# HGRN scores within a chunk: six levels computed in blocks of 32 tokens with 32-column weights, kept in a compact matrix and put in place by ScalarE

## The chip, the cores and the metric

The kernel runs on one core of one Trainium2 chip. Its time is the time of one execution on the device in microseconds (us). The engines are TensorE (PE, whose weight loads are shown apart as PEld), VectorE (DVE), ScalarE (ACT), GpSimd (POOL) and SyncE (SP, which issues most DMAs).

## The reference, cut to what the change touches

The program is a decoder trunk of two layers over 1024 tokens of width 1024. Layer 0 mixes tokens by HGRN2, layer 1 by a gated linear recurrence, and each is followed by a SwiGLU feed-forward block. The change touches the score part of HGRN2 alone, which is, for each of 8 heads with 128 keys:

```python
rel = bb[:, :, :, None, :] - bb[:, :, None, :, :]          # bb: running sum of log f over the tokens
decay = jnp.exp(jnp.where(causal, rel, -jnp.inf))
scores = jnp.einsum('bhtk,bhtsk,bhsk->bhts', qb, decay, kb)
o = jnp.einsum('bhts,bhsv->bhtv', scores, vb) + jnp.einsum('bhtk,bhkv->bhtv', qb * jnp.exp(bb), state)
```

The score of a query at token t and a key at token s carries the product of the forget factors f between them, for each key dimension apart, so it isn't one matrix product.

## The kernel before

**Tiling.** Activations stand transposed, 128 features on the partitions and 512 tokens (a half of the sequence) along the row. A head and a half make one unit: there are 8 x 2 = 16 of them. `unit` makes the projections f, q and g of a head by `gemm` (L275 to L282): three products of fp32r halves for each of 8 row blocks, 128x512 each, so that fp32 accuracy comes out of them. Then it starts a `core` (the function that the change edits).

**The levels.** A core handles 4 chunks of 128 tokens (CPH = 4) by eight levels. Level 0 is a product of keys and queries for the diagonal alone (L485). Levels m = 1, 2, 4, ..., 64 join neighbouring blocks of m tokens: queries in the second half of each pair of blocks against keys in its first half. Up to m = 32 a level is, for each chunk, one full fp32 product: all 128 keys of the chunk are the weights, the 64 queries in second halves are what moves through (L501). Of the 128x64 result only the blocks of that level are wanted, and VectorE copies them under a mask into the score matrix `at` (128 keys x 4 chunks x 128 queries) by COPY_PREDICATED (L532; L486 for level 0). At m = 64 the weights are the 64 keys of the first half alone, the result stands on partitions 0 to 63 (L514), and ScalarE puts it in place (L536). After each level's product VectorE multiplies the keys `kt` and queries `qp` by the running decay products, so it waits for the product, and the next level's product waits for it. A product of fp32 shows in the trace as two pairs of weight load (LDWEIGHTS) and MATMUL, so a level of 4 products is 8 pairs.

**Order.** A core is a generator. Each `gemm` step advances a count of nanoseconds (`tick`), and a core's next level is written out once its count has come up (G_LV = 1300 per level). The instructions of TensorE keep the order in which they are written, so a level of small products stands between 128x512 products of the projections of another head or half. Masks are made once by GpSimd (`make_mask`) behind the first unit's values. After the last level the keys are transposed (L543), the state is updated (L552 and the lines behind it), and the output is the product of `at` with the values (L566).

Of the kernel before, what the change touches and what calls it, by code (L numbers as in the profile page):

```python
# [9 lines left out]
F32 = mybir.dt.float32  # L10
F32R = mybir.dt.float32r
I32 = mybir.dt.int32
U8 = mybir.dt.uint8
AF = mybir.ActivationFunctionType
ALU = mybir.AluOpType
P = 128
H = 512
EPS = 1e-6
GELU_C = 0.7978845608028654
N_ST, N_OUT = 7000.0, 1500.0  # L20
N_T = 1000.0
# [26 lines left out]
def tile_trunk(  # L48
# [23 lines left out]
    nc = tc.nc  # L72
# [3 lines left out]
    CPH = H // P  # L76
# [39 lines left out]
    def pe(ins):  # L116
        return keep(ins)
# [3 lines left out]
    make_identity(nc, ident[:])  # L121
    ones = cp.tile([P, P], F32, name="ones")
    nc.vector.memset(ones[:], 1.0)
    identi = cp.tile([P, P], U8, name="identi")
    nc.vector.tensor_copy(identi[:], ident[:])
    masks = {}

    def make_mask(m):
        mf = t2k("D", f"mf{m}")[:, :P]
        keep(nc.gpsimd.memset(mf, 0.0))  # L130
        v = mf.rearrange("p (b h m) -> p b h m", h=2, m=m)[:, :, 1, :]
        keep(nc.gpsimd.memset(v, 1.0))
        nb = P // (2 * m)
        keep(
            nc.gpsimd.affine_select(
                out=v, in_=v, pattern=[[-2 * m, nb], [0, m]], compare_op=ALU.is_ge, fill=0.0, base=0, channel_multiplier=1
            )
        )
        keep(
            nc.gpsimd.affine_select(  # L140
                out=v, in_=v, pattern=[[2 * m, nb], [0, m]], compare_op=ALU.is_ge, fill=0.0, base=m - 1, channel_multiplier=-1
            )
        )
        mi = cp.tile([P, P], U8, name=f"mask{m}")
        keep(nc.gpsimd.tensor_copy(mi[:], mf))
        masks[m] = mi

# [317 lines left out]
    def hgrn(norms, after):  # L467
# [2 lines left out]
        operand, side, second, factors, raws, first_cols, loads = norms  # L470
        ws0, omlb = [], []
        ats = [sp.tile([P, CPH, P], F32, tag="slab", name=f"at{i}", bufs=BUFS["slab"]) for i in range(2)]
        n_at = [0]
        state = {}

        def core(h, half, hd, qt, ft, kt, vt, sink, flags):


            nm = f"{h}_{half}"
            ct = lambda a, c: a[:, c * P : (c + 1) * P]  # L480
            at = ats[n_at[0] % 2]
            n_at[0] += 1
            lv = psb(f"lv0_{nm}")
            for c in range(CPH):
                pe(mm(ct(lv, c), ct(kt, c), ct(qt, c), start=True, stop=True))  # L485
            nc.vector.copy_predicated(  # L486
                at[:], identi[:].unsqueeze(1).to_broadcast([P, CPH, P]), lv[:].rearrange("p (c t) -> p c t", t=P)
            )
            qp = t2k("D", f"qp_{nm}")
            tt(qp[:], qt[:], ft[:], ALU.mult)  # L490
            yield G_LV
            Tt = slab(f"T_{nm}")
            T, off, m = ft[:], 0, 1
            while m < P:
                lv = psb(f"lv{m}_{nm}")
                if m < 64:
                    second = lambda a: a.rearrange("p (b h m) -> p b h m", h=2, m=m)[:, :, 1, :]
                    lvc = lambda c: lv[:, c * 64 : (c + 1) * 64]
                    for c in range(CPH):
                        pe(  # L500
                            mm(  # L501
                                lvc(c).rearrange("p (b m) -> p b m", m=m),
                                ct(kt, c),
                                second(ct(qp, c)),
                                start=True,
                                stop=True,
                            )
                        )
                    sel = at[:].rearrange("p c (b h m) -> p c b h m", h=2, m=m)[:, :, :, 1, :]
                    msk = second(masks[m][:]).unsqueeze(1).to_broadcast([P, CPH, P // (2 * m), m])  # L510
                else:
                    for c in range(CPH):
                        pe(
                            mm(  # L514
                                lv[0:64, c * 64 : (c + 1) * 64],
                                kt[:, c * P : c * P + 64],
                                qp[:, c * P + 64 : (c + 1) * P],
                                start=True,
                                stop=True,
                            )  # L520
                        )
                n2 = H // (2 * m)
                Tv = T.rearrange("p (n h) -> p n h", h=2)
                qv = qp[:].rearrange("p (n h m) -> p n h m", h=2, m=m)[:, :, 1, :]
                kv = kt[:].rearrange("p (n h m) -> p n h m", h=2, m=m)[:, :, 0, :]
                tt(kv, kv, Tv[:, :, 1:2].to_broadcast([P, n2, m]), ALU.mult)
                tt(qv, qv, Tv[:, :, 0:1].to_broadcast([P, n2, m]), ALU.mult)
                Tn = Tt[:, off : off + n2]
                off += n2
                tt(Tn, Tv[:, :, 0], Tv[:, :, 1], ALU.mult)  # L530
                if m < 64:
                    nc.vector.copy_predicated(  # L532
                        sel, msk, lv[:, : CPH * 64].rearrange("p (c b m) -> p c b m", c=CPH, m=m)
                    )
                else:
                    nc.scalar.copy(at[0:64, :, 64:P], lv[0:64, : CPH * 64].rearrange("p (c t) -> p c t", t=64))  # L536
                T, m = Tn, 2 * m
                yield G_LV


            pk = psb(f"pk_{nm}")
            for c in range(CPH):
                pe(nc.tensor.transpose(ct(pk, c), ct(kt, c), ident[:]))  # L543
            kT = slab(f"kT_{nm}")
            act(kT[:], pk[:], AF.Copy)
            yield G_PK
            pu = psb(f"pu_{nm}")
            vs = lambda c: vt[c // 2][:, (c % 2) * 2 * P + hd * P : (c % 2) * 2 * P + (hd + 1) * P]
            Ss = [state.get(h)]
            St = slab(f"S_{nm}")  # L550
            for c in range(CPH):
                pe(mm(ct(pu, c), ct(kT, c), vs(c), start=True, stop=True))  # L552
            for c in range(CPH):
                if half == NHALF - 1 and c == CPH - 1:
                    continue
                S1 = ct(St, c)
                if Ss[-1] is None:
                    nc.vector.tensor_copy(S1, ct(pu, c))
                else:
                    stt(S1, Ss[-1], T[:, c : c + 1], ct(pu, c), ALU.mult, ALU.add)  # L560
                Ss.append(S1)
            state[h] = Ss[-1]
            yield G_PU
            po = psb(f"po_{nm}")
            for c in range(CPH):
                pe(mm(ct(po, c), at[:, c, :], vs(c), start=True, stop=Ss[c] is None))  # L566
                if Ss[c] is not None:
                    pe(mm(ct(po, c), ct(qp, c), Ss[c], start=False, stop=True))

            sq = t2k("A", f"osq_{nm}")  # L570
            act(sq[:], po[:], AF.Square)
            ss = sp.tile([P, CPH], F32, tag="ss", name=f"ss_{nm}")
            nc.vector.tensor_reduce(
                ss[:], sq[:].rearrange("p (c v) -> p c v", v=P), mybir.AxisListType.X, ALU.add
            )
            rs = rsqrt(f"o{nm}", ss[:], 1.0 / P, CPH)
            on = slab(f"on_{nm}")
            tt(
                on[:].rearrange("p (c v) -> p c v", v=P),
                po[:].rearrange("p (c v) -> p c v", v=P),  # L580
                rs.unsqueeze(2).to_broadcast([P, CPH, P]),
                ALU.mult,
            )
            flags["tail"] = True
            yield G_PL if h == NH - 1 and half else G_PO
            while "g" not in flags:
                yield 600.0
            pt = psb(f"pt_{nm}")
            for c in range(CPH):
                pe(nc.tensor.transpose(ct(pt, c), ct(on, c), ident[:]))  # L590
            og = t2k("B", f"og_{nm}")
            stt(og[:], pt[:], pc("hn", 0), flags["g"][:], ALU.mult, ALU.mult)
            sink[half] = split(f"o{nm}", og[:])
# [145 lines left out]
        for h in range(NH):  # L739
# [5 lines left out]
            if hd == 0:  # L745
                wv = value_weights(hp) if h else []
                if h == 0:
                    vts = [values_start(wv)]
                    for m in (1, 2, 4, 8, 16, 32):
                        make_mask(m)  # L750
                    for a in ats:
                        keep(nc.gpsimd.memset(a[:], 0.0))
                    factors.job = start(second())
                else:
                    vts = [values(hp, half, wv) for half in range(NHALF)]
# [851 lines left out]
```

## Time and profile before

| what | us |
|---|---|
| median of 3 runs (lowest, highest) | 2274.61 (2270.29, 2275.03) |
| profiled execution: its own time | 2269.08 |
| profiled execution: span of the core | 2267.4 |
| TensorE busy | 2224.9 |
| TensorE weight loads busy | 1868.1 |
| VectorE busy | 1628.9 |
| ScalarE busy | 936.1 |
| GpSimd busy | 840.5 |

Busy time of TensorE is the union of its matmuls, whose ends are modelled, so it is not a share of its peak. The HGRN units run from about 50 us to 606 us of the span; the rest is the feed-forward blocks and the second layer, which the change leaves alone. Columns of the views are named where the rows stand.

### The profile page before, as it was taken

How to read it: one execution, taken by the hardware profiler on the slowest of the kernel's cores; microseconds unless marked ns; L12 is line 12 of the kernel's file. 1: busy time of each engine (PE TensorE's matmuls, PEld its weight loads, DVE VectorE, ACT ScalarE, POOL GpSimd, SP SyncE). 2: the span in 40 equal slices, each digit the busy share in tenths (PEclk: the TensorE clock that was granted, in tenths of full speed). 3: DMA queues.
4: the chain of work that ended last, by engine and by line, in shares of the span. 5: the costliest groups of instructions: out<-in, count | busy, mean ns of one | idle time of the engine just before them, and what ended most of it. 6: DMA issues, size and time to landing. Idle time of an engine off the chain costs nothing.

```text
span 2267.4 us, 31380 instructions
## 1 busy us (share of the span) xinstructions
PE 2224.9 (98%) x11022; PEld 1868.1 (82%) x11022; DVE 1628.9 (72%) x2667; ACT 936.1 (41%) x1559; POOL 840.5 (37%) x603
## 2 busy tenths in 40 slices
PE   8999999999999999999999999998999999999998
PEld 8898898898887888888888887877887888888887
DVE  7676758758888776766666767767987777675666
ACT  6223122222353333333544365567733333345444
POOL 4102011012206775654324333234056766543240
PEclk9999999999999999999999999999999999999999
DMA  5013123212444555444776111111645645447762
GB/s 150 28 48 112 56 66 103 80 61 75 154 167 158 188 188 161 156 156 154 279 258 221 43 38 47 47 56 56 209 135 191 198 155 172 141 156 283 260 203 76
DMA packets 279072, 310.94 MB, mean 137 GB/s; under 512 B 18953, under 2 KB 166530, under 8 KB 278914
## 3 DMA queue, kind: packets, MB, share of 16 engines
q1 hardware_dynamic: 278914, 308.94, 41.7%
q8 instruction: 86, 1.41, 0.3%
q14 instruction: 72, 0.59, 0.1%
HBM read 216.07 MB, written 92.80 MB: 136 GB/s over the span
## 4 chain that ended last, share of the span: by engine, by line
PE 86%; DVE 8%; ACT 3%; issue 1%; DMA 1%; SPq 0%; POOL 0%; DVEq 0%; ACTq 0%; POOLq 0%
PE pa L279 8%; PE pa L280 8%; PE pa L281 8%; PE pb L279 4%; PE pb L280 4%; PE pb L281 4%; PE lv L501 3%; PE pc L279 3%; PE pc L281 3%; PE pc L280 3%; PE pg L279 2%; PE pg L280 2%; PE pg L281 2%; PE pd L281 1%; PE pd L280 1%; PE pd L279 1%
## 5 line engine op out<-in xcount | busy, mean ns | idle before, releaser
L1119 POOL TENSOR_TENSOR s<-raw_fi,raw_fi 128x512 f32<-128x512 f32 x40 | 57.9, 1448 | 283.4 <-DMA raw_fi<-in_ffn_w_in_dram 274.2
L93 DVE TENSOR_TENSOR lo_a<-raw_fi,hi_a 128x512 fp32r<-128x512 f32 x116 | 117.7, 1016 | 43.9 <-ACT hi_a L93 43.9
L93 DVE TENSOR_TENSOR lo_s<-s,hi_s 128x512 fp32r<-128x512 f32 x80 | 93.4, 1168 | 75.4 <-ACT hi_s L93 75.1
L279 PE MATMUL pa<-hi_x,hi_w 128*128 128x512 f32 (+1 forms) x364 | 139.7, 384 | 0.0
L281 PE MATMUL pa<-hi_x,lo_w 128*128 128x512 f32 (+1 forms) x364 | 139.1, 382 | 0.0
L280 PE MATMUL pa<-lo_x,hi_w 128*128 128x512 f32 (+1 forms) x364 | 139.1, 382 | 0.0
L93 DVE TENSOR_TENSOR lo_x<-ld_t,hi_x 128x512 fp32r<-128x512 f32 x88 | 87.0, 997 | 56.0 <-ACT hi_x L93 37.1
L204 POOL TENSOR_TENSOR lo_w<-ld_s,hi_w 128x512 fp32r<-128x512 f32 x44 | 69.0, 1569 | 150.6 <-ACT hi_w L93 103.2
L93 ACT ACTIVATE hi_a<-raw_fi 128x512 fp32r<-128x512 f32 x116 | 72.8, 627 | 123.5 <-PE pc L280 76.7
L279 PE MATMUL pa<-hi_t_n,hi_s 128*128 128x512 f32 x304 | 119.6, 394 | 3.1 <-ACT u L93 1.5
L280 PE MATMUL pa<-lo_t_n,hi_s 128*128 128x512 f32 x304 | 118.4, 389 | 0.0
L281 PE MATMUL pa<-hi_t_n,lo_s 128*128 128x512 f32 x304 | 118.4, 389 | 0.0
L501 PEld LDWEIGHTS lv<-qp,k 128*128 128x128 f32 x768 | 98.6, 191 | 8.8 <-issue 1.5
L279 PE MATMUL pb<-hi_x,hi_w 128*128 128x512 f32 x264 | 102.7, 389 | 0.0
L280 PE MATMUL pb<-lo_x,hi_w 128*128 128x512 f32 x264 | 102.7, 389 | 0.0
L281 PE MATMUL pb<-hi_x,lo_w 128*128 128x512 f32 x264 | 102.7, 389 | 0.0
L501 PE MATMUL lv<-qp,k 128*128 128x64 f32 x768 | 96.5, 268 | 1.3 <-DVE qp L93 1.2
L204 POOL TENSOR_TENSOR lo_f<-raw_f,hi_f 128x512 fp32r<-128x512 f32 x14 | 18.3, 1311 | 211.6 <-DMA wls<-lo_was 88.8
L93 ACT ACTIVATE hi_s<-s 128x512 fp32r<-128x512 f32 x80 | 50.6, 632 | 108.1 <-PE pa L280 76.3
L93 DVE TENSOR_TENSOR lo_s<-raw_fi,hi_s 128x512 fp32r<-128x512 f32 x80 | 94.9, 1186 | 0.1
L93 ACT ACTIVATE hi_w<-ld_s 128x512 fp32r<-128x512 f32 x88 | 55.3, 628 | 78.7 <-PE pb L280 24.5
L93 ACT ACTIVATE hi_s<-raw_fi 128x512 fp32r<-128x512 f32 x80 | 50.2, 628 | 79.5 <-PE pd L280 57.0
(398 smaller groups left out, 7289.4 us busy)
## 6 DMA issues: line engine op xcount, KB each, us to landing
raw_fi<-in_ffn_w_in_dram SPq DMA_DIRECT2D x160, 256.0 KB, 3.2
da<-in_ffn_w_out_dram SPq DMA_DIRECT2D x88, 256.0 KB, 3.9
ld_a<-in_ffn_w_out_dram SPq DMA_DIRECT2D x66, 256.0 KB, 4.8
xd<-xT SPq DMA_DIRECT2D x32, 256.0 KB, 2.5
xT<-xd SPq DMA_DIRECT2D x32, 256.0 KB, 4.8
hb22d<-c SPq DMA_DIRECT2D x22, 256.0 KB, 3.3
ht3d<-c SPq DMA_DIRECT2D x22, 256.0 KB, 2.7
ht2d<-c SPq DMA_DIRECT2D x22, 256.0 KB, 2.0
```

What stands on the lines that cost most here:

```text
L93: ins = f(*args, **kwargs)
L204: ins = (lo_engine.tensor_tensor if lo_engine else tt)(lo[:], src, hi[:], ALU.subtract)
L279: pe(mm(pt, wh, xh, start=st[0], stop=False, skip_group_check=skip))
L280: pe(mm(pt, wh, xl, start=False, stop=False, skip_group_check=skip))
L281: pe(mm(pt, wl, xh, start=False, stop=st[1], skip_group_check=skip))
L501: mm(lvc(c).rearrange("p (b m) -> p b m", m=m), ct(kt, c), second(ct(qp, c)), start=True, stop=True,)
L1119: add(s1, a21, a22, ALU.add)
```

## The change

A block length BL = 32 is introduced. For level 0 and the levels m = 1 to 16 the new helper `within` takes each chunk in four blocks of 32 tokens: 32 keys are the weights, the 32 queries of the same block (level 0) or the 16 of them in second halves (m = 1 to 16) move through, and the result goes to the 32 partitions of those keys. A level is then 16 products where it was 4. Level m = 32 becomes, for each chunk, two products of 32 keys by 32 queries (8 products where there were 4). Level m = 64 stays as it was: 4 products of 64 keys by 64 queries.

The results of levels 0 to 16 go by COPY_PREDICATED into a new compact matrix `ad` (128 x 4 x 32), a quarter of `at`; the masks and the identity shrink to 32 columns. After level 16 ScalarE copies `ad` in four pieces of 32 partitions onto the diagonal of `at`, and level 32 goes into `at` by two ScalarE copies, without VectorE and without a mask. GpSimd makes five masks, each cut out by four copies, and the identity by four, and clears `ad` too.

```diff
+    identi = cp.tile([P, BL], U8, name="identi")
     masks = {}
+
+    def own_columns(o, src):
+        for b in range(0, P, BL):
+            keep(nc.gpsimd.tensor_copy(o[b : b + BL, :], src[b : b + BL, b : b + BL]))
...
+        ads = [cp.tile([P, CPH, BL], F32, name=f"ad{i}") for i in range(2)]
...
             lv = psb(f"lv0_{nm}")
-            for c in range(CPH):
-                pe(mm(ct(lv, c), ct(kt, c), ct(qt, c), start=True, stop=True))
+
+            def within(q, n):
+
+                for c in range(CPH):
+                    for b in range(0, P, BL):
+                        t = slice(c * P + b, c * P + b + BL)
+                        o, qs = lv[b : b + BL, c * n : (c + 1) * n], q(t)
+                        if len(qs.shape) == 3:
+                            o = o.rearrange("p (b m) -> p b m", m=qs.shape[2])
+                        pe(mm(o, kt[:, t], qs, start=True, stop=True))
+
+            within(lambda t: qt[:, t], BL)
             nc.vector.copy_predicated(
-                at[:], identi[:].unsqueeze(1).to_broadcast([P, CPH, P]), lv[:].rearrange("p (c t) -> p c t", t=P)
+                ad[:],
+                identi[:].unsqueeze(1).to_broadcast([P, CPH, BL]),
+                lv[:, : CPH * BL].rearrange("p (c t) -> p c t", t=BL),
             )
...
-                if m < 64:
+                if m < BL:
                     second = lambda a: a.rearrange("p (b h m) -> p b h m", h=2, m=m)[:, :, 1, :]
-                    lvc = lambda c: lv[:, c * 64 : (c + 1) * 64]
+                    within(lambda t: second(qp[:, t]), BL // 2)
+                    sel = ad[:].rearrange("p c (b h m) -> p c b h m", h=2, m=m)[:, :, :, 1, :]
+                    msk = second(masks[m][:]).unsqueeze(1).to_broadcast([P, CPH, BL // (2 * m), m])
+                else:
+
                     for c in range(CPH):
...
+                        for b in range(0, P, 2 * m):
+                            k0, q0 = c * P + b, c * P + b + m
+                            o = lv[b : b + m, c * m : (c + 1) * m]
+                            pe(mm(o, kt[:, k0 : k0 + m], qp[:, q0 : q0 + m], start=True, stop=True))
...
-                if m < 64:
+                if m < BL:
                     nc.vector.copy_predicated(
-                        sel, msk, lv[:, : CPH * 64].rearrange("p (c b m) -> p c b m", c=CPH, m=m)
+                        sel, msk, lv[:, : CPH * BL // 2].rearrange("p (c b m) -> p c b m", c=CPH, m=m)
                     )
+                    if 2 * m == BL:
+                        for b in range(0, P, BL):
+                            nc.scalar.copy(at[b : b + BL, :, b : b + BL], ad[b : b + BL, :, :])
                 else:
-                    nc.scalar.copy(at[0:64, :, 64:P], lv[0:64, : CPH * 64].rearrange("p (c t) -> p c t", t=64))
+                    for b in range(0, P, 2 * m):
+                        src = lv[b : b + m, : CPH * m].rearrange("p (c t) -> p c t", t=m)
+                        nc.scalar.copy(at[b : b + m, :, b + m : b + 2 * m], src)
```

On TensorE, where head 0's second half (names `_0_1`) runs its level m = 16 between two steps of a 128x512 projection (`pg`), there stands before:

```order
L280 MATMUL pg_0_1213<-lo_x_0_149,hi_g_0_1098 128x512
L281 MATMUL pg_0_1213<-hi_x_0_148,lo_g_0_1099 128x512
L501 MATMUL lv_0_1_1217<-qp_1_1120,k_1_891 128x64 x4
L279 MATMUL pg_0_1213<-hi_x_1_159,hi_g_0_1098 128x512
L280 MATMUL pg_0_1213<-lo_x_1_160,hi_g_0_1098 128x512
```

and in the changed kernel:

```order
L284 MATMUL pg_0_1369<-lo_x_0_150,hi_g_0_1194 128x512
L285 MATMUL pg_0_1369<-hi_x_0_149,lo_g_0_1195 128x512
L499 MATMUL lv_0_1_1373<-qp_1_1228,k_1_966 32x16 x16
L283 MATMUL pg_0_1369<-hi_x_1_160,hi_g_0_1194 128x512
L284 MATMUL pg_0_1369<-lo_x_1_161,hi_g_0_1194 128x512
```

The level stands at the same place; 4 products of 64 moving columns have become 16 of 16 columns, each with its own weights.

On ScalarE, around the end of the same core (the copies into `at_`), there stands before:

```order
L93 ACTIVATE k_0_1106<-k_0_1106 128x512
L93 ACTIVATE sg_q_0_1209<-q_0_1164 128x512
L536 COPY at_136<-lv_0_1_1253 64x4x64
L93 ACTIVATE sg_g_0_1266<-g_0_1212 128x512
L93 ACTIVATE kT_1_1282<-pk_1_1277 128x512
```

and in the changed kernel:

```order
L94 ACTIVATE k_0_1202<-k_0_1202 128x512
L94 ACTIVATE sg_q_0_1365<-q_0_1296 128x512
L541 COPY at_135<-ad_137 32x4x32 x4
L545 COPY at_135<-lv_0_1_1407 32x4x32 x2
L545 COPY at_135<-lv_0_1_1430 64x4x64
L94 ACTIVATE sg_g_0_1443<-g_0_1368 128x512
L94 ACTIVATE kT_1_1459<-pk_1_1454 128x512
```

Six copies have come in ahead of the one that was there, between the two sigmoids of the next head.

On VectorE, around the levels m = 16 and m = 32 of that core, there stands before:

```order
L532 COPY_PREDICATED at_136<-mask_463,lv_0_1_1217 128x16x16
L93 TENSOR_TENSOR qp_0_1290<-q_0_1164,f_0_1160 128x512 [waits DVE_49]
L93 TENSOR_TENSOR k_1_891<-k_1_891,T_1_1131 128x8x32 [waits PE_49]
L93 TENSOR_TENSOR qp_1_1120<-qp_1_1120,T_1_1131 128x8x32 [waits DVE_49]
L532 COPY_PREDICATED at_136<-mask_470,lv_0_1_1235 128x8x32 [waits DVE_49]
L93 TENSOR_TENSOR k_1_891<-k_1_891,T_1_1131 128x4x64 [waits DVE_49,PE_49]
```

and in the changed kernel:

```order
L536 COPY_PREDICATED ad_137<-mask_476,lv_0_1_1373 128x4x16
L94 TENSOR_TENSOR qp_0_1479<-q_0_1296,f_0_1292 128x512 [waits DVE_49]
L94 TENSOR_TENSOR k_1_966<-k_1_966,T_1_1239 128x8x32 [waits PE_49]
L94 TENSOR_TENSOR qp_1_1228<-qp_1_1228,T_1_1239 128x8x32 [waits DVE_49]
L94 TENSOR_TENSOR k_1_966<-k_1_966,T_1_1239 128x4x64 [waits DVE_49,PE_49]
```

The masked copy of level 16 covers 64 elements per partition where it covered 256, and that of level 32 is gone.

## Rows read from the trace of the kernel before

**Rows 1.** The page, part 1: busy us (share of the span) xinstructions.

```profile
span 2267.4 us, 31380 instructions
PE 2224.9 (98%) x11022; PEld 1868.1 (82%) x11022; DVE 1628.9 (72%) x2667; ACT 936.1 (41%) x1559; POOL 840.5 (37%) x603
```

**Rows 2.** The page, part 4: the chain that ended last, by engine.

```profile
PE 86%; DVE 8%; ACT 3%; issue 1%; DMA 1%; SPq 0%; POOL 0%; DVEq 0%; ACTq 0%; POOLq 0%
```

**Rows 3.** Windows, 40 to 620 us: engines' busy us (instructions), granted clock, DMA share, GB/s.

```profile
40.00:620.00 580.00, 573.71 (x3600) 505.45 (x3600) 414.85 (x1029) 154.16 (x269) 82.40 (x62) 1.00 0.24 76
```

**Rows 4.** Waits of TensorE, 40 to 620 us: us in total, times, longest.

```profile
PE pt L590 <- DVE on L93: 1.8, 2, 1.5
PE po L568 <- DVE S L93: 1.3, 2, 0.7
PE lv L501 <- DVE qp L93: 1.2, 3, 0.7
PE lv L485 <- DVE q L93: 1.0, 1, 1.0
PE pu L552 <- ACT kT L93: 0.7, 1, 0.7
```

**Rows 5.** Timeline of TensorE: start us, us, engine, line, operation, out<-in, xcount.

```profile
590.94 0.39 PE L281 MATMUL ho<-hi_o,lo_ho 128*128 128x512 f32 x1
591.17 1.00 PE L501 MATMUL lv<-qp,k 128*128 128x64 f32 x8
591.98 0.48 PE L279 MATMUL ho<-hi_o,hi_ho 128*128 128x512 f32 x1
592.29 0.39 PE L280 MATMUL ho<-lo_o,hi_ho 128*128 128x512 f32 x1
592.52 0.40 PE L281 MATMUL ho<-hi_o,lo_ho 128*128 128x512 f32 x1
...
593.91 0.40 PE L281 MATMUL ho<-hi_o,lo_ho 128*128 128x512 f32 x1
594.24 0.68 PE L514 MATMUL lv<-qp,k 128*64 128x64 f32 x8
594.84 0.50 PE L279 MATMUL ho<-hi_o,hi_ho 128*128 128x512 f32 x1
595.18 0.40 PE L280 MATMUL ho<-lo_o,hi_ho 128*128 128x512 f32 x1
```

**Rows 6.** Timeline with the weight loads, at two other places.

```profile
196.15 0.19 PEld L279 LDWEIGHTS pf<-hi_x,hi_f 128*128 128x128 f32 x1
196.18 0.48 PE L279 MATMUL pf<-hi_x,hi_f 128*128 128x512 f32 x1
...
240.57 0.54 PEld L514 LDWEIGHTS lv<-qp,k 128*64 128x64 f32 x8 [0.36 <-issue]
```

**Rows 7.** The tile lv: duration ns min/median/max, first and last start us.

```profile
L501 PE MATMUL lv<-qp,k x768: 217/275/323, 53.6 to 591.9; 128*128 128x64 f32 x192
L485 PE MATMUL lv<-q,k x128: 270/275/377, 51.3 to 569.5; 128*128 128x128 f32 x128
L514 PEld LDWEIGHTS lv<-qp,k x128: 132/138/138, 69.8 to 594.6; 128*64 128x64 f32 x128
```

**Rows 8.** Groups of VectorE and ScalarE, 40 to 620 us: busy us, mean ns; idle before.

```profile
L532 DVE COPY_PREDICATED at<-mask,lv 128x256 f32<-128x256 uint8 x96 | 50.9, 530 | 0.0
L486 DVE COPY_PREDICATED at<-identi,lv 128x512 f32<-128x512 uint8 x16 | 11.7, 733 | 1.2 <-PE lv L485 1.2
L536 ACT COPY at<-lv 64x256 f32<-64x256 f32 x16 | 5.8, 365 | 36.9 <-PE lv L514 31.0 <-DVE raw_wa L1046 5.7
```

**Rows 9.** GpSimd: its last mask copies' group, then the timeline where it stops and goes on.

```profile
L145 POOL CAST mask<-mf 128x128 uint8<-128x128 f32 x6 | 2.1, 358 | 0.4
35.41 0.99 POOL L752 MEMSET at<- 128x512 f32 x2
60.44 2.77 POOL L204 TENSOR_TENSOR lo_f<-raw_f,hi_f 128x512 fp32r<-128x512 f32 x2 [24.04 <-ACT hi_f L93]
```

More of the change, by code (lines that the diff above doesn't have):

```diff
@@ L18 @@
 EPS = 1e-6
+BL = 32
 GELU_C = 0.7978845608028654
@@ L123, in tile_trunk @@
     nc.vector.memset(ones[:], 1.0)
-    identi = cp.tile([P, P], U8, name="identi")
-    nc.vector.tensor_copy(identi[:], ident[:])
+    identi = cp.tile([P, BL], U8, name="identi")
     masks = {}
+    def own_columns(o, src):
+        for b in range(0, P, BL):
+            keep(nc.gpsimd.tensor_copy(o[b : b + BL, :], src[b : b + BL, b : b + BL]))
     def make_mask(m):
@@ L143, in make_mask @@
         )
-        mi = cp.tile([P, P], U8, name=f"mask{m}")
-        keep(nc.gpsimd.tensor_copy(mi[:], mf))
-        masks[m] = mi
+        masks[m] = cp.tile([P, BL], U8, name=f"mask{m}")
+        own_columns(masks[m], mf)
     xT = {}
@@ L481, in core @@
             at = ats[n_at[0] % 2]
+            ad = ads[n_at[0] % 2]
             n_at[0] += 1
             lv = psb(f"lv0_{nm}")
-            for c in range(CPH):
-                pe(mm(ct(lv, c), ct(kt, c), ct(qt, c), start=True, stop=True))
+            def within(q, n):
[7 more added lines that the diff above has]
+            within(lambda t: qt[:, t], BL)
             nc.vector.copy_predicated(
-                at[:], identi[:].unsqueeze(1).to_broadcast([P, CPH, P]), lv[:].rearrange("p (c t) -> p c t", t=P)
+                ad[:],
+                identi[:].unsqueeze(1).to_broadcast([P, CPH, BL]),
+                lv[:, : CPH * BL].rearrange("p (c t) -> p c t", t=BL),
             )
@@ L495, in core @@
                 lv = psb(f"lv{m}_{nm}")
-                if m < 64:
+                if m < BL:
                     second = lambda a: a.rearrange("p (b h m) -> p b h m", h=2, m=m)[:, :, 1, :]
-                    lvc = lambda c: lv[:, c * 64 : (c + 1) * 64]
[L499 to L510, printed above, removed]
+                    within(lambda t: second(qp[:, t]), BL // 2)
+                    sel = ad[:].rearrange("p c (b h m) -> p c b h m", h=2, m=m)[:, :, :, 1, :]
+                    msk = second(masks[m][:]).unsqueeze(1).to_broadcast([P, CPH, BL // (2 * m), m])
                 else:
                     for c in range(CPH):
[L513 to L521, printed above, removed]
+                        for b in range(0, P, 2 * m):
+                            k0, q0 = c * P + b, c * P + b + m
+                            o = lv[b : b + m, c * m : (c + 1) * m]
+                            pe(mm(o, kt[:, k0 : k0 + m], qp[:, q0 : q0 + m], start=True, stop=True))
                 n2 = H // (2 * m)
@@ L748, in hgrn @@
                     vts = [values_start(wv)]
-                    for m in (1, 2, 4, 8, 16, 32):
+                    for m in (1, 2, 4, 8, 16):
                         make_mask(m)
-                    for a in ats:
+                    own_columns(identi, ident)
+                    for a in ats + ads:
                         keep(nc.gpsimd.memset(a[:], 0.0))
```

## The prediction

> **What bounds the kernel now.** I read part 1 of the page first: TensorE is busy for 2224.9 of 2267.4 us, VectorE for 72% [rows 1]. The chain that ended last lies on TensorE for 86% and on VectorE for 8% [rows 2]. The levels run from 51 to 595 us [rows 7], so the stage is read from the window of 40 to 620 us: TensorE 573.71 of 580.00 us, VectorE 414.85, ScalarE 154.16, GpSimd 82.40, the granted clock 1.00, which is the upper of its two levels, 2.4 GHz [rows 3]. Last, what TensorE waited for there: five kinds of wait, 1.8 + 1.3 + 1.2 + 1.0 + 0.7 = 6.0 us in all, 5.3 of them for VectorE [rows 4]. So in this stage TensorE is the bound; a us that its instructions take more is a us of the kernel, and all that the other engines can give back is at most these 6 us.
>
> **What a level costs TensorE today.** Busy time is no measure of it, since matmuls overlap; I take starts. A level stands between 128x512 products that start 0.23 us apart (592.29 to 592.52) [rows 5]. From the start of the product ahead (590.94) to that of the second product behind (592.29) pass 1.35 us; two products of 0.23 us are in it, so the level costs 1.35 - 0.46 = 0.89 us [rows 5]. That is 8 pairs of weight load and matmul at 0.89 / 8 = 0.111 us. Level 0 has the same 8 pairs and twice the moving columns with the same 275 ns for a matmul [rows 7], and I take 0.89 us for it too: the 128-column weight load sets the pace, not the moving side.
>
> **What a narrow level costs.** The level m = 64 has already what the change brings to the others: weights of 64 columns and results on a part of the partitions. From 593.91 to 595.18 pass 1.27 us, less 0.46 it is 0.81 us [rows 5]. Its 8 weight loads last 0.54 us from first start to last end, one takes 138 ns, so they are (0.54 - 0.138) / 7 = 0.057 us apart [rows 6, 7]. Seven such steps are 0.40 us; the other 0.81 - 0.40 = 0.41 us is a fixed price of getting in and out: the level starts 0.33 us after the product ahead instead of 0.23, and the next 128x512 product starts 0.34 us ahead of its follower (594.84 to 595.18) after a gap behind the last small one [rows 5]; the weight load waits 0.36 us for nothing that the profile names [rows 6]. A full level pays no such price: 8 x 0.111 is its whole 0.89. So a level of n pairs with narrow weights costs 0.41 + (n - 1) s, where s is the spacing of pairs.
>
> **The change part by part.**
>
> *Pairs.* A product of fp32 is two pairs (768 matmuls for 6 levels x 16 units x 4 chunks = 384 products [rows 7]). Levels 0 to 16, six of them in 16 units, 96 in all, go from 8 pairs to 32; level 32, 16 in all, from 8 to 16; level 64 stays.
>
> *Spacing s of 32-column pairs.* No row shows it. From 128 to 64 columns the spacing fell from 0.111 to 0.057 us, 0.027 us for 32 columns; the same step again gives 0.030 us. The shortest distance from a weight load to its matmul that the timeline shows is also 0.03 us (196.15 to 196.18) [rows 6]. This is what I take. The upper end is 0.057 us, the nearest row itself: nothing gained below 64 columns, if the rate at which instructions come is what holds there. The lower end is a quarter of 0.030, 0.0075 us, if the four column groups on which successive blocks lie work side by side.
>
> *Sum on TensorE at 0.030.* A level of 32 pairs: 0.41 + 31 x 0.030 = 1.34 us, 0.45 more than 0.89, times 96 is +43.2 us. Level 32: 0.41 + 15 x 0.030 = 0.86 us, times 16 is -0.5 us. Together +42.7 us. At 0.057: 2.18 and 1.27 us, (1.29 x 96) + (0.38 x 16) = +130 us. At 0.0075: 0.64 and 0.52 us, -(0.25 x 96) - (0.37 x 16) = -30 us. The balance is at (0.89 - 0.41) x 112 / (31 x 96 + 15 x 16) = 0.0167 us.
>
> *VectorE.* Masked copies of 256 elements take 530 ns, of 512 elements 733 ns [rows 8]. The line through the two gives some 0.38 us for 64 elements and 0.43 us for 128; in proportion to the elements it would be 0.13 and 0.18 us. 80 copies then save 0.15 to 0.40 us each, 16 of level 0 save 0.30 to 0.55, and 16 of level 32 save all of their 530 ns: 25 to 49 us of VectorE's work. It reaches the end only through the waits above, so it is worth 0 to 6 us. Each level's product also ends later, by 0.45 us, and VectorE's updates of keys and queries wait for it, which eats into the same slack. I take -2 us.
>
> *ScalarE.* Six copies more in a unit, 96 in all, at no more than the 365 ns of the 64x256 copy [rows 8]: at most 35 us in a stage in which it has 426 us free [rows 3]. The copies of `ad` wait for the masked copy of level 16 on VectorE, and behind them in ScalarE's queue stand the copies of level 32 and 64, the sigmoid of the next gate and the transposed keys `kT`, for which TensorE waited 0.7 us once [rows 4]. At most 6 x 0.365 = 2.2 us of delay in a unit, covered by the 128x512 products written between; uncovered in every unit it would be 35 us, and I take nothing.
>
> *GpSimd.* 24 mask copies for 6 at 358 ns or less are up to 6.4 us more, and two small clears. It is done at 36.4 us and idle for 24 us before 60.44 [rows 9], and level 0 is first written at 51.3 us [rows 7]: covered. The identity's copy moves to it from VectorE's first microseconds, worth nothing.
>
> **The sum.** 2269.1 us of the profiled execution + 42.7 - 2 = 2310 us for an execution like it. The median of the three runs is 5.5 us above that execution, so I forecast 2315 us.
>
> **Rivals.**
>
> *The column groups overlap (faster).* Four successive blocks of 32 keys put their results on four different groups of 32 partitions. Below 0.0167 us of spacing the kernel gains; with four loads side by side it is -30 - 2 us, 2243 us. For it: nothing in the trace, since level 64 puts all its results on the same partitions. Against it: each fp32 product is two pairs on the same group, one after the other, so at best every second load finds another group free. With half the loads hidden s is 0.015 us and the sum -5.5 - 2 us, 2267 us. The Trainium skill, page "TensorEngine Tiling (Array Packing)", section "Key Properties", says that different tiles can run weight loads and matmuls in parallel; by that rule it would be this rival, and no run so far shows it. Against that stands the Trainium skill's "TensorE: Matmul & The Clock Gate", Part 1, by which starts of matmuls never come closer than about 25 ns; by that alone, an estimate from the page, the sum on TensorE would be +27 us. I give 0.13 to a gain of over 0.2%.
>
> *Partial overlap.* s between 0.016 and 0.024 us gives -4 to +21 us, 2270 to 2296 us: 0.15, of which 0.06 lies within 0.2%.
>
> *The narrow pairs come no faster than today's (far slower).* Each pair is two instructions and a wide level has 16 of them in 0.89 us, the narrow one 16 in 0.81; none shows 64 in about a microsecond. If the instruction stream holds at 0.057 us, it is +130 - 2 us, 2403 us. For 0.042 us and more I give 0.15. Against it: the spacing of 64-column pairs lies on the weight load's own slope (0.84 ns a column from 128 to 64), which leaves no sign of a floor at 0.057.
>
> *VectorE was the bound after all.* Then the 25 to 49 us saved there would pay for much of the loss. The 6.0 us of TensorE's waits [rows 4] speak against it, and it is in the sum with 2.
>
> **How the numbers follow.** Forecast, s from 0.024 to 0.042 us, +21 to +79 us: 0.57. Far slower: 0.15. Partial overlap: 0.15. Overlap with a gain: 0.13. A difference of over 0.2% (4.5 us) is about what a measurement of this kernel can tell from none. Slower by more than that: 0.57 + 0.15 + 0.09 = 0.81; the same: 0.06; faster: 0.13. For the range I leave out spacings below 0.0155 us (about 0.12) and above 0.054 us (about 0.07): 2268 to 2395 us.
>
> **What would show it.** In the trace after, the small levels of lines 499 and 525 should show 32 matmuls in about 1.0 us (16 in 0.5), and from the product ahead to the second behind 1.8 us where there are 1.35 now. TensorE should still be busy for 98%, its waits in the stage no more than 6 us, and the stage longer by about 41 us; the masked copies should take 0.2 to 0.4 us, with no effect on the end. Levels that take under 0.9 us net would refute the spacing, and with it the sign. A fixed price other than 0.41 us moves the sum by 11 us for each 0.1 us.

## The result and the profile after

The changed kernel takes 2237.19 us (median of 4 runs, 2235.83 to 2237.62), the kernel before 2272.45 us in the same comparison (4 runs, 2268.57 to 2275.03). The ratio is 0.9842, with a 95% interval from 0.9828 to 0.9856: faster by 35 us. I had forecast 2315 us, 40 us above the 2274.6 us known then. The profiled execution took 2237.62 us, 31.5 less than that of before (2269.08).

The page of the changed kernel, part 1 and the engines of part 4, against [rows 1, 2]:

```profile
span 2235.9 us, 36324 instructions
PE 2189.1 (98%) x13454; PEld 1803.0 (81%) x13454; DVE 1591.2 (71%) x2650; ACT 959.6 (43%) x1655; POOL 843.3 (38%) x619
...
PE 85%; DVE 9%; ACT 3%; issue 1%; DMA 1%; POOL 0%; SPq 0%; DVEq 0%; ACTq 0%; POOLq 0%
```

TensorE has 2432 matmuls more and is busy for 36 us less. It is the bound as before, at the same share of the span.

TensorE in the changed kernel, the same kind of timeline as [rows 5] (start us, us, engine, line, operation, out<-in, xcount). First a level of 16 tokens or fewer, with the row of its weight loads, then a level of 32 tokens:

```profile
221.75 0.40 PE L285 MATMUL ho<-hi_o,lo_ho 128*128 128x512 f32 x1
222.08 0.45 PE L499 MATMUL lv<-qp,k 128*32 128x16 f32 x32
222.45 0.50 PE L283 MATMUL ho<-hi_o,hi_ho 128*128 128x512 f32 x1
222.79 0.39 PE L284 MATMUL ho<-lo_o,hi_ho 128*128 128x512 f32 x1
...
222.08 0.35 PEld L499 LDWEIGHTS lv<-qp,k 128*32 128x32 f32 x32 [0.37 <-issue]
...
224.40 0.39 PE L285 MATMUL ho<-hi_o,lo_ho 128*128 128x512 f32 x1
224.72 0.45 PE L525 MATMUL lv<-qp,k 128*32 128x32 f32 x16
225.10 0.50 PE L283 MATMUL ho<-hi_o,hi_ho 128*128 128x512 f32 x1
225.43 0.39 PE L284 MATMUL ho<-lo_o,hi_ho 128*128 128x512 f32 x1
```

Read as the prediction reads [rows 5], from the product ahead to the second behind, less two products of 0.23 us: the level of 32 pairs costs 222.79 - 221.75 - 0.46 = 0.58 us and the level of 16 pairs 225.43 - 224.40 - 0.46 = 0.57 us, where a level of 8 wide pairs cost 0.89. The 32 matmuls start and end within 0.45 us, one lasts 0.183 (below), so they start (0.45 - 0.183) / 31 = 0.0086 us apart. A column group is here the 32 output partitions that a block's result goes to; there are four. The 16 of level 32, on two column groups, start (0.45 - 0.196) / 15 = 0.017 us apart.

The tile lv of the changed kernel (duration ns min/median/max, first and last start), against [rows 7], and then the groups of ScalarE and VectorE between 40 and 620 us (busy us, mean ns), against [rows 8]:

```profile
L499 PEld LDWEIGHTS lv<-qp,k x2560: 106/113/113, 53.6 to 555.3; 128*32 128x32 f32 x197
L499 PE MATMUL lv<-qp,k x2560: 176/183/204, 53.6 to 555.3; 128*32 128x16 f32 x197
L499 PE MATMUL lv<-q,k x512: 189/196/217, 51.6 to 537.7; 128*32 128x32 f32 x171
...
L541 ACT COPY at<-ad 32x128 f32<-32x128 f32 x64 | 18.9, 296 | 29.6 <-DVE ad L536 29.1
L545 ACT COPY at<-lv 32x128 f32<-32x128 f32 x32 | 8.1, 254 | 1.0 <-PE lv L525 0.8
...
L536 DVE COPY_PREDICATED ad<-mask,lv 128x64 f32<-128x64 uint8 x80 | 19.8, 248 | 0.0
L502 DVE COPY_PREDICATED ad<-identi,lv 128x128 f32<-128x128 uint8 x16 | 4.7, 295 | 0.3 <-PE lv L499 0.2
```

The last level starts at about 560 us where it was 595. By their durations the masked copies fell from 50.9 + 11.7 = 62.6 to 19.8 + 4.7 = 24.5 us. ScalarE's 96 new copies are 18.9 + 8.1 = 27.0 us.

The window of 40 to 620 us (columns as in [rows 3]) and TensorE's longest waits between 40 and 600 us, against [rows 4]:

```profile
40.00:620.00 580.00, 570.75 (x6187) 467.55 (x6187) 408.33 (x1070) 201.25 (x403) 85.84 (x70) 1.00 0.27 87
...
PE pt L599 <- DVE on L94: 2.4, 4, 1.7
PE lv L525 <- DVE ad L536: 1.8, 2, 1.0
PE po L577 <- DVE S L94: 1.3, 3, 0.8
PE lv L499 <- DVE q L94: 1.0, 1, 1.0
PE lv L525 <- DVE qp L94: 0.9, 1, 0.9
```

The waits grew from 6.0 to some 9 us: with shorter levels VectorE is late a little more often. The granted clock of this stretch is still 1.00.

The stage's end shows in the last products of the projection `ho`, first of before, then of after (columns as in the tile view above):

```profile
L281 PE MATMUL ho<-hi_o,lo_ho x128: 388/393/398, 215.1 to 641.1; 128*128 128x512 f32 x128
...
L285 PE MATMUL ho<-hi_o,lo_ho x128: 388/392/398, 204.0 to 608.0; 128*128 128x512 f32 x128
```

So the stage of the kernel before ends at 641.1 us of the span, and not at the 606 us given ahead of the prediction, and that of the changed kernel at 608.0.

**Where the 31.5 us lie.** Over all levels that stand between 128x512 products (81 of the 112 that the change narrows), the median cost of a wide one was 0.903 us and is 0.576 now, for 32 pairs and for 16 (two products taken at 0.453 us, unrounded). I take the other 31 levels to have gained as much. The difference of 0.327 us times 96 + 16 levels is -36.6 us on TensorE. From the first level's start to the last of these products were 589.8 us and are 556.4: -33.4, because TensorE's idle time in the stage rose from 6.3 to 9.2 us. The program behind it took 1627.9 us after 1626.2, in code that the change leaves alone. So -36.6 + 2.9 + 1.7 = -32.0, against 31.5 measured.

### The profile page after: what moved, and what is told of

Its sections match the earlier page's. It is cut to its first block, busy times and chain, and to the rows that moved or that the text cites. A ratio compares the mean times of both kernels' runs of the same rounds, so it can differ in the third digit from the quotient of the medians.

```text
span 2235.9 us, 36324 instructions
## 1 busy us (share of the span) xinstructions
PE 2189.1 (98%) x13454; PEld 1803.0 (81%) x13454; DVE 1591.2 (71%) x2650; ACT 959.6 (43%) x1655; POOL 843.3 (38%) x619
## 4 chain that ended last, share of the span: by engine, by line
PE 85%; DVE 9%; ACT 3%; issue 1%; DMA 1%; POOL 0%; SPq 0%; DVEq 0%; ACTq 0%; POOLq 0%
PE pa L283 8%; PE pa L284 8%; PE pa L285 8%; PE pb L283 4%; PE pb L284 4%; PE pb L285 4%; PE pc L283 3%; PE pc L285 3%; PE pc L284 3%; PE pg L283 2%; PE pg L284 2%; PE pg L285 2%; PE pd L285 1%; PE pd L284 1%; PE pd L283 1%; PE pv L283 1%
## 5 line engine op out<-in xcount | busy, mean ns | idle before, releaser
L285 PEld LDWEIGHTS pa<-hi_x,lo_w 128*128 128x128 f32 x364 | 68.4, 188 | 13.4
L284 PEld LDWEIGHTS pa<-lo_x,hi_w 128*128 128x128 f32 x364 | 68.4, 188 | 13.2
```

The lines of the kernel that those rows point to most:

```text
L284: pe(mm(pt, wh, xl, start=False, stop=False, skip_group_check=skip))
L285: pe(mm(pt, wl, xh, start=False, stop=st[1], skip_group_check=skip))
```

## The experiments

In the expectations, theory A says that the pairs gain because loads and matmuls for four column groups go on side by side; theory B says that small pairs come fast by themselves, whatever the group. Level costs below are medians over all levels between 128x512 products, read as above.

### Does the order of the groups matter?

The same products, the two loops exchanged: all eight pairs of a column group come in a row.

```diff
-                for c in range(CPH):
-                    for b in range(0, P, BL):
+                for b in range(0, P, BL):
+                    for c in range(CPH):
```

> The changed kernel with the two loops of the helper swapped: blocks outside, chunks inside. The same products, the same result; but four products in a row now put their results on the same 32 partitions, where the changed kernel goes to another group of 32 partitions with every product. Theory A (the column groups work side by side; loads into one group come one after another at the 0.030 us that I forecast): a level of 32 pairs takes 0.31 + 31 x 0.030 = 1.24 us where it takes 0.58, 96 levels, so +64 us on 2237 us: about 2301 us, and 32 matmuls about 30 ns apart. Theory B (32-column pairs are quick by themselves, 8.5 ns, wherever the result goes): no change, 2237 us. Something between, if TensorE looks past the pairs that are held up.

Measured 2275.45 us (2271.39 to 2281.55), ratio 1.0011 [1.0, 1.0023]: the whole gain is gone, by the order alone. The timeline of TensorE in this kernel:

```profile
225.67 0.40 PE L285 MATMUL ho<-hi_o,lo_ho 128*128 128x512 f32 x1
226.00 0.89 PE L499 MATMUL lv<-qp,k 128*32 128x16 f32 x32
226.81 0.50 PE L283 MATMUL ho<-hi_o,hi_ho 128*128 128x512 f32 x1
227.15 0.39 PE L284 MATMUL ho<-lo_o,hi_ho 128*128 128x512 f32 x1
```

A level costs 227.15 - 225.67 - 0.46 = 1.02 us. The starts one by one say why it isn't the 1.24 us of theory A: within a group the loads follow each other by 28 to 32 ns, but the next group's first load starts when three matmuls of the group ahead are still outstanding (152 ns after the level's start, with its matmul at 154; the last of the eight matmuls of the group ahead starts at 243 ns). Mean spacing 22.6 ns. So the side by side of the groups is shown, and so is a short look ahead past pairs that are held up. Theory B falls.

### How far does TensorE look ahead?

Two chunks of a group in a row (four pairs), then the next group:

```diff
-                for c in range(CPH):
-                    for b in range(0, P, BL):
+                for c, b in [(c0 + i, b) for c0 in (0, 2) for b in range(0, P, BL) for i in range(2)]:
+                    if True:
```

> The changed kernel with another order of the same products: two chunks of one block in a row, then the next block (groups 0,0,1,1,2,2,3,3, twice). With all four chunks in a row the level took 1.02 us, with none in a row 0.58. If TensorE takes pairs strictly in order: within a group 31 ns, 7 ns at a change of group, so three of four steps at 31 ns, 25 ns on average, 1.09 us a level, +49 us on 2237: 2286 us. If it looks past held-up pairs by about four pairs (what the changes of group in the run with four in a row look like): two groups side by side, 16 ns, 0.81 us, +22 us: 2260 us. If it looks further ahead: 8.5 ns, 2237 us.

Measured 2239.98 us (2238.33 to 2242.74), ratio 0.9857 [0.9843, 0.987], level 0.622 us. Its row of TensorE:

```profile
223.82 0.48 PE L499 MATMUL lv<-qp,k 128*32 128x16 f32 x32
```

The 32 matmuls take 0.48 us where the changed kernel takes 0.45; they start 9.5 ns apart. Four pairs in a row on one group are looked past with little loss (the first matmuls of the level start at 0, 13, 27 and 40 ns), eight are not. This is the further look ahead of the expectation. Together with the run before it fits a group that holds about three pairs behind the one at work; that is read off the starts, and no run isolates it.

### Four groups against two

Blocks of 64 tokens: weights of 64 columns, two column groups, 16 pairs in a level.

```diff
-BL = 32
+BL = 64
...
-        ads = [cp.tile([P, CPH, BL], F32, name=f"ad{i}") for i in range(2)]
+        ads = [cp.tile([P, CPH, BL], F32, name="ad")] * 2
...
-                    for m in (1, 2, 4, 8, 16):
+                    for m in (1, 2, 4, 8, 16, 32):
...
-                    for a in ats + ads:
+                    for a in ats + ads[:1]:
```

> The changed kernel with blocks of 64 tokens instead of 32 (levels 0 to 32 by products of 64 keys on two groups of 64 partitions; one compact matrix for both units instead of two, for room). A level then has 16 pairs with 64-column loads. Theory A: loads of 64 columns were 57 ns apart on one group, on two groups they go side by side, 29 ns: 0.31 + 15 x 0.029 = 0.74 us a level against 0.58, 112 levels: +19 us, 2256 us. Theory B (narrowness alone sets the spacing): 57 ns as in level 64, 1.17 us a level, +66 us, 2303 us.

One matrix `ad` serves both cores here, so where two cores run interleaved their results mix in it, which leaves TensorE's work as it is. VectorE's masked copies are twice as wide as in the changed kernel, and level 32 has one again; the level's cost is read on TensorE alone. Measured 2259.59 us (2257.27 to 2264.93), ratio 0.9942 [0.9922, 0.9962]. TensorE's timeline:

```profile
222.51 0.39 PE L285 MATMUL ho<-hi_o,lo_ho 128*128 128x512 f32 x1
222.83 0.66 PE L499 MATMUL lv<-qp,k 128*64 128x32 f32 x16
223.41 0.50 PE L283 MATMUL ho<-hi_o,hi_ho 128*128 128x512 f32 x1
223.75 0.39 PE L284 MATMUL ho<-lo_o,hi_ho 128*128 128x512 f32 x1
```

A level costs 223.75 - 222.51 - 0.46 = 0.78 us (median 0.789), the matmuls start 29.1 ns apart: half of the 58 ns of a 64-column load on one group. Theory A had put 0.74 us and 2256 us. So the spacing is one load's time divided by the groups at work: 58 / 2 = 29, 31 / 4 = 8 (8.5 measured), and 31 / 2 = 16 for level 32 of the changed kernel (16.6 measured).

### The price of getting in and out

Each level of the blocks written in two parts of two chunks; a product of the projections can come between them.

```diff
-            def within(q, n):
-
-                for c in range(CPH):
+            def within(q, n, cs=range(CPH)):
+
+                for c in cs:
...
-            within(lambda t: qt[:, t], BL)
+            within(lambda t: qt[:, t], BL, (0, 1))
+            yield 0.0
+            within(lambda t: qt[:, t], BL, (2, 3))
...
-                    within(lambda t: second(qp[:, t]), BL // 2)
+                    within(lambda t: second(qp[:, t]), BL // 2, (0, 1))
+                    yield 0.0
+                    within(lambda t: second(qp[:, t]), BL // 2, (2, 3))
```

> The changed kernel with each level 0 to 16 written in two parts of two chunks, with a step of the 128x512 products between them: the same products, but TensorE goes in and out of narrow weights 96 times more. If the fixed price of a level (0.31 us in the changed kernel) is that of going in and out, +0.30 us each: +29 us, 2266 us. If it is a start of the level's own that is paid once, nothing: 2237 to 2240 us.

Measured 2277.42 us (2273.94 to 2280.43), ratio 1.002 [1.001, 1.003]: 40 us more than the changed kernel. TensorE's timeline around one half of a level:

```profile
223.56 0.40 PE L285 MATMUL ho<-hi_o,lo_ho 128*128 128x512 f32 x1
223.88 0.32 PE L499 MATMUL lv<-qp,k 128*32 128x16 f32 x16
224.13 0.50 PE L283 MATMUL ho<-hi_o,hi_ho 128*128 128x512 f32 x1
224.47 0.39 PE L284 MATMUL ho<-lo_o,hi_ho 128*128 128x512 f32 x1
```

Half a level costs 224.47 - 223.56 - 0.46 = 0.45 us (median 0.458), and 16 pairs at 9.1 ns account for 0.14 of it. Cost and pairs of the halves and of the whole levels agree on a fixed price: 0.458 - 15 x 0.0091 = 0.32 and 0.576 - 31 x 0.0085 = 0.31 us. Written in two, a level pays it twice: 2 x 0.458 - 0.576 = 0.34 us more, times 96 is +32.6 us. The stage is 592.2 us long, 35.8 more than in the changed kernel. TensorE's idle time in it rose too (9.2 to 14.3 us), and two stretches of it ran at a lower clock, of which the last experiment tells more; a few levels were not split, so 32.6 is the upper end of the price. The program behind the stage, the same code, took 7.4 us more. The expected 2266 us had the price alone.

Next, levels 0 and 1 in one piece, so that one price in each unit is saved:

```diff
+            qp = t2k("D", f"qp_{nm}")
+            tt(qp[:], qt[:], ft[:], ALU.mult)
+            yield G_LV
             lv = psb(f"lv0_{nm}")
...
-            qp = t2k("D", f"qp_{nm}")
-            tt(qp[:], qt[:], ft[:], ALU.mult)
-            yield G_LV
```

> The changed kernel with the products of level 0 written directly ahead of those of level 1 (level 1 needs only q times f beside what level 0 needs), so that each unit goes in and out of narrow weights once less. By the fixed price of 0.31 us a time: 16 x 0.31 = -5 us on 2237: 2232 us. If the fixed price is not that of going in and out: 2237 us.

Measured 2236.92 us (2232.99 to 2241.01), ratio 0.9842 [0.9826, 0.9858]: not to be told from the changed kernel. Where the two levels stand between 128x512 products (12 of the 16 units) they cost 0.887 us together, 0.589 + 0.576 apart: 0.28 us are saved by one visit less, so the price is there. From the first level to the last product the stage is 3.8 us shorter (552.6 after 556.4), but its first level starts 1.9 us later, so it ends only 1.8 us sooner. TensorE's idle time in it rises from 9.2 to 11.0 us; of the waits that the profile lists, those for ScalarE's `kT` grew from 0.7 to 1.6 us and those for VectorE from 8.0 to 8.6.

### Level 64 on two groups

The odd chunks of level 64 put their results on partitions 64 to 127, those of level 32 on the two groups that were free.

```diff
-                            o = lv[b : b + m, c * m : (c + 1) * m]
+                            r = b + m * (c % 2)
+                            o = lv[r : r + m, (c // 2) * m : (c // 2 + 1) * m]
...
-                        src = lv[b : b + m, : CPH * m].rearrange("p (c t) -> p c t", t=m)
-                        nc.scalar.copy(at[b : b + m, :, b + m : b + 2 * m], src)
+                        for odd in range(2):
+                            r = b + m * odd
+                            src = lv[r : r + m, : CPH // 2 * m].rearrange("p (c t) -> p c t", t=m)
+                            nc.scalar.copy(at[b : b + m, odd::2, b + m : b + 2 * m], src)
```

> The changed kernel with the odd chunks of level 64 on partitions 64 to 127 and the odd chunks of level 32 on the groups that stood free (ScalarE's copies shift them back, in twice as many pieces). By the column groups: level 64, 8 pairs at 29 ns on two groups for 58 ns on one, 0.35 + 7 x 0.029 = 0.55 us for 0.81; level 32, 16 pairs at 8.5 ns on four groups for 16.6 on two, 0.44 for 0.58: 16 x (0.26 + 0.14) = -6 us, 2231 us. By narrowness alone: nothing, 2237 us.

Measured 2234.16 us (2231.44 to 2238.37), ratio 0.9836 [0.9821, 0.9851]. TensorE's timeline around level 64:

```profile
225.42 0.39 PE L285 MATMUL ho<-hi_o,lo_ho 128*128 128x512 f32 x1
225.74 0.45 PE L526 MATMUL lv<-qp,k 128*64 128x64 f32 x8
226.12 0.50 PE L283 MATMUL ho<-hi_o,hi_ho 128*128 128x512 f32 x1
226.45 0.39 PE L284 MATMUL ho<-lo_o,hi_ho 128*128 128x512 f32 x1
```

Level 64 falls from 0.809 to 226.45 - 225.42 - 0.46 = 0.57 us (median 0.582), and level 32 from 0.576 to 0.462. The products, their operands and their order are the very same here, only the output partitions differ, so the gain of these levels is that of the groups. That is 16 x (0.227 + 0.114) = 5.5 us, and the stage is 5.5 us shorter (550.9 after 556.4). In the time of the program 3 us of it are left, which the intervals don't separate from nothing.

Both of the last two edits together:

> The two edits before in one kernel: if both prices are right they add up, -11 us on 2237: 2226 us. If VectorE or ScalarE hold the levels by then, less: 2232 us.

Measured 2235.50 us (2232.61 to 2238.72), ratio 0.9836 [0.9823, 0.9849]; the stage ends 7.3 us sooner than in the changed kernel (1.8 and 5.4 for the edits alone), and the total shows 2 us of it. The program behind the stage, the same code in all of these, took 1630.2 us here, 1629.8 and 1631.2 in the two single edits, and 1627.9 in the changed kernel: it differs between executions with the stretches of lower granted clock in it (in windows of 10 us, the time lost to them up to 2220 us of the span is 3.4 us in the changed kernel's profile and 8.5 to 8.9 us in these three). No version measured beats the changed kernel by more than its uncertainty.

### What VectorE's relief is worth, in the kernel before and in the changed one

The kernel before without its two masked copies:

```diff
-            nc.vector.copy_predicated(
-                at[:], identi[:].unsqueeze(1).to_broadcast([P, CPH, P]), lv[:].rearrange("p (c t) -> p c t", t=P)
-            )
...
-                if m < 64:
-                    nc.vector.copy_predicated(
-                        sel, msk, lv[:, : CPH * 64].rearrange("p (c b m) -> p c b m", c=CPH, m=m)
-                    )
-                else:
+                if m == 64:
```

> The kernel before without VectorE's masked copies of levels 0 to 32 (the scores within 64 tokens are left out; TensorE's work stays). It takes 63 us of VectorE's work away, more than the change does. If the gain of the change came through TensorE: at most the 6 us of TensorE's waits, 2266 to 2272 us. If it came through VectorE: some 30 us or more, 2245 us or below.

Measured 2270.95 us (2269.3 to 2276.97), ratio 0.9992 [0.9983, 1.0001]. Its window, columns as in [rows 3]:

```profile
40.00:620.00 580.00, 574.10 (x3601) 506.62 (x3600) 366.09 (x917) 154.25 (x270) 82.65 (x62) 1.00 0.24 76
```

VectorE is busy for 366.09 us instead of 414.85. These are 48.8 us less and not the 63 of the expectation, which added up durations: successive instructions of VectorE overlap (in the kernel before a masked copy of 0.44 us starts at 133.93 us and the next instruction at 134.27). The kernel gains some 2 us, which the interval doesn't separate from nothing. In the kernel before, VectorE's work is covered.

The changed kernel with each masked copy done three times, which gives VectorE back a good part of what it had lost:

```diff
-                    nc.vector.copy_predicated(
-                        sel, msk, lv[:, : CPH * BL // 2].rearrange("p (c b m) -> p c b m", c=CPH, m=m)
-                    )
+                    for _ in range(3):
+                        nc.vector.copy_predicated(
+                            sel, msk, lv[:, : CPH * BL // 2].rearrange("p (c b m) -> p c b m", c=CPH, m=m)
+                        )
```

> The changed kernel with each of the 80 masked copies of levels 1 to 16 made three times over (the same values): 160 copies of 0.22 us more, 35 us of VectorE's work put back, about what the change took away. If the gain came through TensorE alone: 0 to 6 us more than 2237, by the waits of TensorE for VectorE in the stage: 2237 to 2243 us. If VectorE's relief carries the gain or a good part of it: 2255 us or more.

Measured 2247.50 us (2245.86 to 2252.07), ratio 0.9891 [0.9872, 0.991]: 10 us of the 35 are gone, more than TensorE alone allowed for and less than a kernel bound by VectorE would show. The group of these copies and TensorE's two largest waits, then a stretch of TensorE's timeline, windows of 2 us around it, and the window from the first level to the last product of `ho` of the kernel before, the changed kernel and this one (windows: columns as in [rows 3]):

```profile
L537 DVE COPY_PREDICATED ad<-mask,lv 128x64 f32<-128x64 uint8 x240 | 60.1, 250 | 1.7
...
PE lv L525 <- DVE ad L537: 4.3, 3, 2.5
PE lv L525 <- DVE qp L94: 3.4, 1, 3.4
...
199.46 0.39 PE L285 MATMUL pg<-hi_x,lo_g 128*128 128x512 f32 x1
202.33 0.45 PE L525 MATMUL lv<-qp,k 128*32 128x32 f32 x16 [2.48 <-DVE ad L537]
...
204.42 0.63 PE L283 MATMUL pg<-hi_x,hi_g 128*128 128x512 f32 x1
204.85 0.63 PE L284 MATMUL pg<-lo_x,hi_g 128*128 128x512 f32 x1
205.27 0.63 PE L285 MATMUL pg<-hi_x,lo_g 128*128 128x512 f32 x1
...
202.00:204.00 2.00, 1.67 (x22) 1.42 (x23) 2.00 (x8) 0.94 (x4) 0.00 (x0) 0.98 0.76 218
204.00:206.00 2.00, 2.00 (x7) 1.16 (x6) 0.45 (x1) 0.75 (x3) 0.00 (x0) 0.50 0.66 221
...
51.30:641.10 589.80, 583.51 (x3626) 512.78 (x3625) 424.15 (x1045) 158.41 (x275) 82.40 (x62) 1.00 0.25 81
51.60:608.00 556.40, 547.15 (x6058) 447.06 (x6057) 387.65 (x1028) 182.74 (x371) 83.26 (x62) 1.00 0.27 87
51.50:616.70 565.20, 549.66 (x6057) 449.50 (x6057) 412.90 (x1189) 183.12 (x371) 84.89 (x62) 0.99 0.27 86
```

By their durations the copies are 60.1 - 19.8 = 40 us more, about the 38 that the change had taken away. By busy time, in the last three rows, the change took 424.15 - 387.65 = 36.5 us from VectorE in the stage, and 412.90 - 387.65 = 25.3 us are put back here, at levels 1 to 16 alone: some two thirds. The levels on TensorE cost the same (0.577 us). The stage is 565.2 us long, 8.8 more than in the changed kernel, and TensorE is idle for 15.5 us in it instead of 9.2. The rows from 199 to 206 us show what else a wait can cost: TensorE stood for 2.48 us, and from 204 us its granted clock was 0.50, that is 1.2 GHz, with products 0.43 us apart instead of 0.23. In the windows of 10 us of this stage there are two such dips, from 200 and from 500 us, each a mean of 0.83, so about 1.7 us lost in each; the second came behind the wait of 3.4 us. The changed kernel has none there. With 6.3 us of idle time they make 9.7 us, near the 8.8.

## Why the prediction was wrong

- **TensorE is the bound: right.** Busy for 98% in both kernels; what the levels gave back on TensorE (36.6 us) came through nearly whole.
- **The cost of a wide level, 0.89 us: right** (median 0.903).
- **The spacing of 32-column pairs: this step failed.** I took 0.030 us; it is 0.0085. What I rejected was the rival in which the four column groups work side by side, on the argument that "each fp32 product is two pairs on the same group, one after the other, so at best every second load finds another group free". No row bore that argument: level 64, my only narrow level, puts everything on one group, so the trace of before had nothing to say on several. The 0.03 us from a weight load to its matmul bore nothing either: it isn't a distance between pairs, nor the shortest one, since the level 64 of [rows 6] has its first load and its first matmul both at 240.57 us. The runs put in its place: within one group the loads are indeed some 30 ns apart (28 to 32, as taken), but groups don't wait for each other, and a second pair on a group that is busy doesn't hold up the pairs behind it (eight in a row do). The exchange of two loops alone turns 0.576 us a level into 1.016. The change of s from 0.030 to what was measured is, in the formula of the sum, -(31 x 0.0215 x 96) - (15 x 0.0134 x 16) = -67 us.
- **The form "fixed price plus n - 1 spacings": right; its size: too large.** 0.41 us is the price of level 64 by the spacing of its loads (0.809 - 7 x 0.058 = 0.40 in the changed kernel too). For 32 columns it is 0.31 us, by the starts of the matmuls, so another -0.1 x 112 = -11 us. Part of this lies in the reading: by the starts of the matmuls, (0.68 - 0.222) / 7 = 0.065 us apart by [rows 5] with 0.222 us for one, level 64 has 0.809 - 7 x 0.065 = 0.35 us. That a full level pays no price I had from 8 x 0.111, which is how the 0.111 was made; the loads of a wide level do start 111 ns apart in the trace of before. With the two corrections +42.7 becomes about -36, which is what TensorE shows.
- **The rival that came true** was the first: I put 2243 us to it, 6 above what was measured, and a chance of 0.13, and my range began only at 2268 (its upper end, by the formula of the sum, is 2392 and not 2395). The rule of the Trainium skill beside it ("TensorEngine Tiling (Array Packing)", section "Key Properties": different tiles run weight loads and matmuls in parallel) holds here, by 8.5 ns against 22.6 ns for the two orders. The rule that I set against it ("TensorE: Matmul & The Clock Gate", Part 1: starts of matmuls not closer than about 25 ns) doesn't hold for matmuls on different groups: they start 6 to 7 ns apart in this trace. Where a page's rule and a measurement differ, the measurement decides.
- **The instruction stream as a limit (far slower): refuted.** 64 instructions of a level start within 0.27 us; 0.057 us a pair is what one group of 64 columns takes, not what the stream gives.
- **VectorE at -2 us: right for the kernel before, not for the kernel that came.** Taking all masked copies from the kernel before is worth some 2 us. In the changed kernel, putting 25.3 of the 36.5 us back costs 10 us, in waits and in stretches at the lower clock, and leaves a gain of 26. So a part of the gain hangs on VectorE's relief: some 10 us by that run, and an estimate only, since the copies put back stand at other places than those taken away. That it is so because the levels became shorter by 0.33 us each, and VectorE's slack behind each level with them, fits the waits (6.0 us before, some 9 after) but is argued, not shown. I had priced a faster VectorE against the waits of a TensorE that I took to become slower.
- **ScalarE and GpSimd at nothing: no sign to the contrary.** The new copies are 27 us of a stage with over 350 free, and TensorE's waits name ScalarE only for 0.7 us, as before. No run isolates them.

## What to carry to other kernels

Small products cost by their order: where successive weights of few columns go to different groups of output partitions, loads run side by side, and the pace here was one load's time divided by the groups. The same products with one group's eight pairs in a row took 22.6 ns a pair for 8.5, and the kernel's whole gain was gone. Going in and out of narrow weights had a price per visit (0.31 us here), so few long visits beat many short ones as long as TensorE is the bound. And where the trace of before has no row for the one resource on which the sign hangs, an argument about how it must work is no reason for a small chance: both ends deserve to stay in the range.

## What the hardware showed

- Matmuls on different column groups start 6 to 7 ns apart, in sets of four that repeat, from the second set on, every 31 to 32 ns, the time between 32-column loads on one group.
- One 32-column load is recorded with 113 ns, a 64-column one with 138, a 128-column one with 191, but the pace on one group is 31, 58 and 111 ns.
- Fixed price of a visit to narrow weights between 128x512 products: 0.31 us at 32 columns and 0.35 at 64, on one group (0.809 - 7 x 0.065) as on two (0.582 - 7 x 0.033), all by the starts of the matmuls. By the Trainium skill's "TensorEngine Tiling (Array Packing)", section "Key Properties", a change of tiling mode drains TensorE; the runs show a price of this kind, not that draining is all of it.
- After a wait of 2.48 us TensorE ran for a stretch at granted clock 0.50 (1.2 GHz), which cost another 1.7 us or so. The program behind the stage has such stretches in every profile taken here, for 3.4 us of loss or more, and gains of a few us in the stage drown in their number.
